# A hybrid gMLP and Mamba-2 trunk on one core: the head's sums move from GpSimd to VectorE and DMA, the decays' stores change queue, and the scans' chunk and the tail get another order

## The chip, the cores and the metric

One core of a Trainium2 chip runs the whole kernel. The metric is the device time of one execution, in microseconds (us). Five engines work beside each other, each through its own list of instructions in order: TensorE (PE, matmuls, with its weight loads shown as PEld), VectorE (DVE), ScalarE (ACT), GpSimd (POOL) and SyncE (SP, which only issues DMAs). ACT and POOL issue DMAs too. Semaphores tie the lists together.

## The reference

`x` is 1024 tokens by 1024 features in float32. Two layers add to it, and an RMSNorm ends the kernel.

```python
def spatial_gating_mixer(h, w_in, ln_w, ln_b, w_s, b_s, w_out):        # layer A
    z, u, v = jnp.split(h @ w_in, 3, axis=-1)                          # 1024 -> 3 x 2048
    v = layernorm(v, ln_w, ln_b)                                       # chunks of 128 tokens, 8 groups
    mixed = jnp.einsum('gts,bcsgd->bctgd', w_causal, v) + b_s...
    return (u * mixed * jax.nn.silu(z)) @ w_out

def ssd_mixer(h, ...):                                                 # layer B, Mamba-2
    z, xbc, dt_raw = ...split of h @ w_in                              # 2048, 4096, 32
    xbc = jax.nn.silu(causal_depthwise_conv(xbc, conv_w, conv_b))      # 4 taps
    x, Bm, Cm = ...xbc; dt = softplus(dt_raw + dt_bias)
    dA_cs = jnp.cumsum(dt * A, axis=2)                                 # in each chunk of 128
    w_ls = (Cm . Bm) * exp(cs_l - cs_s, causal) * dt
    y = w_ls @ x + (Cm @ prev state) * exp(dA_cs) + x * d_skip
    state = state * exp(dA_cs[-1]) + Bm^T (exp(dA_cs[-1] - dA_cs) * dt * x)
    gated = rmsnorm per group of 256 (y * silu(z))
    return gated @ w_out

h = x
h = h + spatial_gating_mixer(rmsnorm(h), ...)
h = h + ssd_mixer(rmsnorm(h), ...)
return rmsnorm(h)
```

## The kernel before

**Products.** Each float32 factor is split into a high half (a rounded copy, `hi`, on ACT) and a low half (the rest, `lo`, mostly on DVE), and each product is three matmuls: high by high, low by high, high by low (`mm3`, lines 134 to 136). On top of that every big product of a block is made with seven half-sized products in place of eight (Strassen's scheme in Winograd's form). So a `Block` has a left side `HS` of seven split matrices (A11, A12, A22 and the sums S1 to S4, `hh` and `hl` in the profile) and a right side of seven split weights (`wh`, `wl`), made of the raw quarters `b[kh, j]` (`wr`) and the sums t1, t2 (`t`).

**Stages.** `head()` (0 to about 92 us) loads x, normalizes it (`sq`, `rs_a`, `rs_b`, `norm`), transposes it (`tr`), forms the seven split matrices and runs the first block of v. The other v blocks run to about 220, the z and u blocks with the spatial mix to 525, the out-projection of layer A to 690, the step into layer B to 775. `blocks()` (to 1030) runs the z blocks and the xbc blocks of layer B, with the steps of `decays()` (softplus, cumulative sums, exp) and the convolution between their units. `scans()` (1033 to 1405) runs 8 groups of 8 chunks; between the chunks' small matmuls stand the projections of the groups still to come (`pj`, tile `ab`) and, in the last seven chunks, product 1 of the out-projection `bo`. `into_end()` runs the products 2, 7, 6, 4, 5, 3 of `bo` and the final norm.

**Order.** The kernel is written under a manual schedule: each engine executes in the order in which the code writes it. Semaphores only hold an instruction back. DMAs issued by SP and by ACT share eight semaphore lanes in turn, so such a DMA also waits for the one issued eight before it, whichever of the two queues issued that; POOL's DMAs have eight lanes of their own. An instruction that waits holds up all behind it on its engine.

**The head's sums.** `s1` to `s4` are the sums of the left side (F[t] holds the transposed rows t, in two halves), `again` rebuilds A12 from its halves, since F's half has been overwritten. t1, t2, the new b[1, 0] (B of product 4) and b[0, 1] (B of product 7) are four sums of weights. POOL does most of both kinds.

**The middle.** In `blocks()` a `unit` first takes one step of `decays()` (`next(small)`), then writes its matmuls. After the exponentials, eight stores write the cumulative sums and their exponentials to HBM (`cs_d`, `ecs_d`), from SP. `last` is a row of the tile that the `ecs_d` stores read.

**A chunk of the scans**, n of 64: `load` and `decay` (exp on ACT) and `tokens` (DVE) make the tiles of a chunk two ahead, `weights` (L1568, DVE) multiplies them one ahead, `pe_b` (L1577 and on, PE) uses them; `update` and `out` (DVE) take PE's result; `drain` runs steps of the convolution (L1282, DVE); `project` writes filler matmuls.

**The tail.** `sum_c`, `group_rstd` (`guess`, `tail`, `put`) and `rb` pass the last group's sums of squares through HBM: `ss_d`, `sv`, `rs_d`, `rb`. `hook_b(n, c)` writes these steps and the loads of the left side (`get`) between the units of `bo`'s products.

Of the kernel before, what the change touches and what calls it, by code (L numbers as in the profile page):

```python
# [29 lines left out]
def kernel(  # L30
# [149 lines left out]
    HS = new_H(("A11", "A12", "A22", "S1", "S2", "S3", "S4"))  # L180

    class Block:
# [104 lines left out]
        def post(self, n, i, parts=(0, 1)):  # L287
            a = self.acc[n][i]
            if n in (1, 6, 7) and 0 in parts:
                if i == 0:  # L290
                    self.u[n] = q4([P, 2, 512], "u")
                nc.scalar.copy(out=self.u[n][:, i], in_=a)  # L292
# [52 lines left out]
    def head():  # L345

        blk = v_block(0)
        V, S, G = nc.vector, nc.scalar, nc.gpsimd
        TTv, TTg = V.tensor_tensor, G.tensor_tensor
# [40 lines left out]
        def hi(name, t, src):  # L390
            S.copy(out=part(name, t)[0], in_=src)

        def lo(name, t, src):
            h_, l_ = part(name, t)
            TTv(out=l_, in0=src, in1=h_.bitcast(F32), op=ALU.subtract)  # L395

        def copy(t, kh):
            S.copy(out=F[t][:, kh], in_=TP[t][kh])
# [8 lines left out]
        def again(t):  # L407

            h_, l_ = part("A12", t)
            TTg(out=F[t][:, 1], in0=h_.bitcast(F32), in1=l_.bitcast(F32), op=ALU.add)  # L410

        def s3(t):
            TTg(out=F[t - 4][:, 0], in0=F[t - 4][:, 0], in1=F[t][:, 0], op=ALU.subtract)

        def s1(t, eng):
            eng(out=F[t][:, 0], in0=F[t][:, 0], in1=F[t][:, 1], op=ALU.add)

        def s2(t):
            TTv(out=F[t][:, 1], in0=F[t][:, 1], in1=F[t - 4][:, 0], op=ALU.subtract)

        def s4(t, eng=TTg):
            eng(out=F[t - 4][:, 1], in0=F[t - 4][:, 1], in1=F[t][:, 1], op=ALU.subtract)
# [3 lines left out]
        blk.t1, blk.t2 = t1, t2  # L426
        xp = [s8([P, 2, D], "xp") for _ in range(2)]
# [8 lines left out]
        for t in range(4, 8):  # L436
            load_x(t, q4([P, D], "xrow") if t < 7 else wr([P, D]))
# [14 lines left out]
        TTg(out=t1, in0=b[0, 1], in1=b[0, 0], op=ALU.subtract)
        TTg(out=t2, in0=b[1, 1], in1=t1, op=ALU.subtract)
# [3 lines left out]
        rs_a(4), rs_b(4), norm(4)  # L457
        hi("A11", 2, TP[2][0]), copy(2, 0), hi("A12", 2, TP[2][1])
        TTg(out=b[1, 0], in0=b[1, 0], in1=t2, op=ALU.subtract)
        TTg(out=b[0, 1], in0=b[1, 1], in1=b[0, 1], op=ALU.subtract)  # L460
        lo("A11", 2, TP[2][0]), lo("A12", 2, TP[2][1])
        hi("A11", 3, TP[3][0]), copy(3, 0), hi("A12", 3, TP[3][1])
        lo("A11", 3, TP[3][0]), lo("A12", 3, TP[3][1])
        norm(5)
        blk.mm(1, 1, False, (0,)), tr(4), blk.mm(1, 1, False, (1,))
        blk.mm(2, 1, False, (0,)), tr(5), blk.mm(2, 1, False, (1,))
        yhi(4, b[1, 0]), hi("A22", 4, TP[4][1]), copy(4, 1), sq(6), sq(7)
        ylo(4, b[1, 0]), lo("A22", 4, TP[4][1])
        copy(4, 0), rs_a(6), blk.post(2, 0), rs_b(6)
# [30 lines left out]
        ylo(5, t1, TTg)  # L500
        s4(4, TTv)
        for t in range(5, 8):
            s4(t)
# [704 lines left out]
    def decays():  # L1208
# [44 lines left out]
        last = dtw[:, 3, :]  # L1253
# [167 lines left out]
    def blocks():  # L1421
# [9 lines left out]
        small, turn, a21 = decays(), [0], rest_a21()  # L1431
# [7 lines left out]
        def unit(b, n, i):  # L1439
# [7 lines left out]
            elif next(small, 0) == 0 and todo and (turn[0] % 2 or len(todo) > 3):  # L1447
# [67 lines left out]
    class Scan:  # L1515
# [55 lines left out]
        def pe_b(self, c, ends=None):  # L1571
# [17 lines left out]
            if ends is not None:  # L1589
                ends.sum_b(sp[:, 256:512])  # L1590
# [68 lines left out]
        def sum_c(self, th):  # L1659
            (nc.sync if self.g < G - 1 else nc.scalar).dma_start(out=ss_d[self.g, th * 512:(th + 1) * 512].rearrange("(h t) -> h t", h=2),  # L1660
                              in_=self.sr[0:65:64])

    def group_rstd(g, t0, n):
# [4 lines left out]
        queue = nc.sync if g < G - 1 else nc.scalar  # L1668
        queue.dma_start(out=sv, in_=ss_d[g, t0:t0 + n].rearrange("(p c) -> p c", c=c))
# [11 lines left out]
        def put():  # L1681
            (nc.sync if g < G - 2 else nc.scalar).dma_start(out=rs_d[g, t0:t0 + n].rearrange("(p c) -> p c", c=c), in_=got[1])
# [287 lines left out]
```

## Time and profile before

| | |
|---|---|
| median of three runs | 1576.33 us (1572.9 to 1581.41) |
| the profiled execution | 1573.5 us, its span 1571.6 us |
| granted TensorE clock in it | 0.983 |
| PE busy | 1488.6 us (95%) |
| DVE, ACT, POOL busy | 1065.0, 782.2, 421.6 us |

How to read a row of the timeline: start, duration (us), engine (a q behind the name is the engine's own queue of DMA issues), line, operation, out <- in, and in brackets the idle time of the engine before it with what ended it. A row of a group gives the count, the busy time, and the mean of one in ns. A row of waits gives the sum, the count and the longest.

### The profile page before, as it was taken

The numbers are of one execution on the slowest core, as the hardware profiler recorded it, in microseconds if no ns is written. First come the engines' busy times: TensorE is split into PE (matmuls) and PEld (weight loads), VectorE is DVE, ScalarE is ACT, GpSimd is POOL, SyncE is SP. The second block draws the span as 40 slices with busy tenths as digits, with TensorE's granted clock in tenths as the row PEclk, the third lists the DMA queues.
The fourth block names the chain that finished last, engine by engine and source line by source line (L and its number), as shares of the span: only waits on it lengthen the run. The fifth ranks groups of instructions, "written<-read, shape, count | busy, mean of one in ns | idle before, by whom it ended". The sixth has DMA issues, their size and how long they took to land.

```text
span 1571.6 us, 21215 instructions
## 1 busy us (share of the span) xinstructions
PE 1488.6 (95%) x7830; PEld 1229.6 (78%) x7830; DVE 1065.0 (68%) x1701; ACT 782.2 (50%) x1251; POOL 421.6 (27%) x441
## 2 busy tenths in 40 slices
PE   5799999999999999999989999999999999987997
PEld 4799998888888888876768888777777776766876
DVE  7976566665666645778726477766776666776976
ACT  4523233322322445666546566656666756755463
POOL 3601110000000023211011313136776666532121
PEclk8999999999999999999999999999999999998999
DMA  5154333233322999947276988776566554678862
GB/s 176 42 185 137 108 99 112 99 107 104 108 92 87 356 243 240 242 126 160 94 166 147 184 176 164 174 230 196 139 169 182 161 158 132 209 261 175 232 129 107
DMA packets 174839, 251.82 MB, mean 160 GB/s; under 512 B 16288, under 2 KB 102928, under 8 KB 171536
## 3 DMA queue, kind: packets, MB, share of 16 engines
q1 hardware_dynamic: 124120, 168.39, 34.6%
q0 software_dynamic: 39520, 63.19, 20.7%
q10 hardware_dynamic: 11096, 18.90, 3.4%
q8 instruction: 62, 1.02, 0.3%
q14 instruction: 41, 0.34, 0.1%
HBM read 185.61 MB, written 51.18 MB: 151 GB/s over the span
## 4 chain that ended last, share of the span: by engine, by line
PE 63%; issue 15%; DVE 10%; ACT 6%; DMA 4%; POOL 1%; ACTq 0%; SPq 0%; POOLq 0%; DVEq 0%
PE acc L136 10%; PE acc L134 9%; PE acc L135 9%; PE ab L134 4%; PE ab L136 4%; PE ab L135 4%; PE ao L135 3%; PE ao L134 3%; PE ao L136 3%; PE yy L1577 2%; PE yy L1581 2%; DVE wl L112 2%; PE bo L135 2%; PE bo L134 2%; PE bo L136 2%
## 5 line engine op out<-in xcount | busy, mean ns | idle before, releaser
L134 PE MATMUL acc<-hh,wh 128*128 128x512 f32 x868 | 341.2, 393 | 7.7 <-ACT u L292 4.4
L136 PE MATMUL acc<-hh,wl 128*128 128x512 f32 x868 | 339.0, 391 | 1.4 <-DVE wl L112 1.4
L135 PE MATMUL acc<-hl,wh 128*128 128x512 f32 x868 | 338.4, 390 | 0.0
L112 DVE TENSOR_TENSOR wl<-wr,wh 128x1024 fp32r<-128x1024 f32 (+1 forms) x97 | 115.6, 1193 | 129.6 <-ACT wh L111 129.4
L134 PEld LDWEIGHTS acc<-hh,wh 128*128 128x128 f32 x868 | 163.5, 188 | 43.1 <-ACT u L292 6.0
L136 PEld LDWEIGHTS acc<-hh,wl 128*128 128x128 f32 x868 | 163.2, 188 | 37.6 <-DVE wl L112 3.7
L135 PEld LDWEIGHTS acc<-hl,wh 128*128 128x128 f32 x868 | 163.5, 188 | 33.1
L292 ACT COPY u<-acc 128x512 f32<-128x512 f32 x117 | 68.0, 583 | 207.1 <-PE acc L136 205.7
L111 ACT CAST wh<-wr 128x1024 fp32r<-128x1024 f32 (+1 forms) x113 | 116.4, 1030 | 98.4 <-PE acc L135 58.8
L136 PE MATMUL acc<-wh,hl 128*128 128x256 f32 x448 | 130.3, 291 | 12.2 <-DVE hl L395 12.1
L134 PE MATMUL ab<-hh,wh 128*128 128x512 f32 x288 | 129.1, 448 | 6.4 <-DVE x L1282 3.8
L134 PE MATMUL acc<-wh,hh 128*128 128x256 f32 x448 | 130.9, 292 | 3.9 <-DVE vt L331 2.5
L135 PE MATMUL acc<-wl,hh 128*128 128x256 f32 x448 | 129.6, 289 | 1.3 <-DVE wl L405 1.3
L136 PE MATMUL ab<-hh,wl 128*128 128x512 f32 x288 | 113.8, 395 | 0.0
L135 PE MATMUL ab<-hl,wh 128*128 128x512 f32 x288 | 112.9, 392 | 0.0
L136 PEld LDWEIGHTS acc<-wh,hl 128*128 128x128 f32 x448 | 88.7, 198 | 13.6 <-DVE hl L395 13.4
L134 PEld LDWEIGHTS acc<-wh,hh 128*128 128x128 f32 x448 | 88.7, 198 | 5.0 <-issue 2.9
L135 PEld LDWEIGHTS acc<-wl,hh 128*128 128x128 f32 x448 | 88.8, 198 | 1.7 <-DVE wl L405 1.5
L134 PE MATMUL bo<-wh,xh 128*128 128x512 f32 x192 | 77.7, 405 | 7.4 <-ACT wh L111 6.6
L112 DVE TENSOR_TENSOR xl<-ya,xh 128x1024 fp32r<-128x1024 f32 x40 | 49.8, 1246 | 51.2 <-ACT xh L111 51.2
L645 POOL DMA_DIRECT2D y_d<-y x8 | 4.4, 548 | 291.4 <-DVE y L642 291.4
L1550 ACT ACTIVATE wl<-wl,tk 128x128 f32<-128x128 f32 x256 | 81.5, 391 | 0.8 <-DMA wl<-cs_d 0.5
(320 smaller groups left out, 3284.3 us busy)
## 6 DMA issues: line engine op xcount, KB each, us to landing
wr<-in_a_w_in_dram SPq DMA_DIRECT2D x48, 512.0 KB, 3.6
wl<-cs_d SPq DMA_DIRECT2D x64, 256.0 KB, 3.5
wr<-in_b_w_in_dram SPq DMA_DIRECT2D x30, 512.0 KB, 7.3
wb<-in_a_w_out_dram SPq DMA_DIRECT2D x10, 1024.0 KB, 12.0
wb<-in_b_w_out_dram SPq DMA_DIRECT2D x10, 1024.0 KB, 7.7
wr<-in_b_w_in_dram SPq DMA_DIRECT2D x36, 256.0 KB, 7.2
v<-v_d SPq DMA_DIRECT2D x8, 1024.0 KB, 5.0
y_d<-y POOLq DMA_DIRECT2D x8, 1024.0 KB, 5.6
```

Of the source, the lines that this page charges most:

```text
L111: nc.scalar.copy(out=hi, in_=src)
L112: return (eng or nc.vector).tensor_tensor(out=lo, in0=src, in1=hi.bitcast(F32), op=ALU.subtract)
L134: nc.tensor.matmul(out=o, lhsT=l[0], rhs=r[0], start=start, stop=False, **kw)
L135: nc.tensor.matmul(out=o, lhsT=l[0], rhs=r[1], start=False, stop=False, **kw)
L136: nc.tensor.matmul(out=o, lhsT=l[1], rhs=r[0], start=False, stop=stop, **kw)
L292: nc.scalar.copy(out=self.u[n][:, i], in_=a)
L645: store = lambda: nc.gpsimd.dma_start(out=y_d[-1], in_=y)
L1550: nc.scalar.activation(wl[:, j, :], wl[:, j, :], AF.Relu, scale=-1.0, bias=tokc(2, c, self.g)[:, j:j + 1])
L1577: nc.tensor.matmul(out=yy[f * 64:(f + 1) * 64, pt * P:(pt + 1) * P], lhsT=w[:, j * 64:(j + 1) * 64], rhs=wl[:, j, :], start=True, stop=True)
L1581: nc.tensor.matmul(out=yy[:, 256 + pt * P:384 + pt * P], lhsT=self.state[c - 1][:, pt * P:(pt + 1) * P], rhs=self.x(3, c), start=True, sto ...
```

## The change

Four places of the code change, with the same products in the same order on PE.

*The head.* t1, t2, the new b[1, 0], s3, s1 and two low halves go to DVE. ACT copies A12's transposed rows into F as well, so that nothing rebuilds them. The rows 4 to 7 are copied with a minus sign, so that all sums are additions; S1 and S2 take the sign back in their halves. The new b[0, 1] is a scaling on ACT and an addition by DMA from HBM, and S4's sums are additions by DMA from SBUF, all in POOL's queue.

```diff
-            TTg(out=F[t][:, 1], in0=h_.bitcast(F32), in1=l_.bitcast(F32), op=ALU.add)
...
-            TTg(out=F[t - 4][:, 0], in0=F[t - 4][:, 0], in1=F[t][:, 0], op=ALU.subtract)
...
+        def sums(eng, *names):
+            for n, t in names:
+                a, c = {3: (F[t - 4][:, 0], F[t][:, 0]), 1: (F[t][:, 0], F[t][:, 1]),
+                        2: (F[t][:, 1], F[t - 4][:, 0]), 4: (F[t - 4][:, 1], F[t][:, 1])}[n]
+                if eng is None:
+                    nc.gpsimd.dma_start(out=a, in_=c, accum_op=ALU.add)
+                else:
+                    eng.tensor_tensor(out=a, in0=a, in1=c, op=ALU.add)
...
-        TTg(out=t1, in0=b[0, 1], in1=b[0, 0], op=ALU.subtract)
-        TTg(out=t2, in0=b[1, 1], in1=t1, op=ALU.subtract)
...
-        TTg(out=b[1, 0], in0=b[1, 0], in1=t2, op=ALU.subtract)
-        TTg(out=b[0, 1], in0=b[1, 1], in1=b[0, 1], op=ALU.subtract)
...
+        TTv(out=t1, in0=b[0, 1], in1=b[0, 0], op=ALU.subtract)
+        rs_b(4), norm(4)
...
+        norm(5), sq(6), sq(7), rs_a(6)
+        TTv(out=t2, in0=b[1, 1], in1=t1, op=ALU.subtract)
+        rs_b(6)
+        TTv(out=b[1, 0], in0=b[1, 0], in1=t2, op=ALU.subtract)
...
-        for t in (4, 5):
-            s3(t), s1(t, TTg)
-        yhi(6, t2)
+        sums(V, (3, 4), (3, 5), (1, 4), (1, 5))
+        S.mul(b[0, 1], b[0, 1], -1.0), blk.add(b[0, 1], 1, 1), yhi(6, t2)
...
-        s3(6), s1(6, TTg), s3(7)
+        sums(V, (2, 4), (2, 5), (3, 6), (1, 6))
...
+        sums(V, (3, 7), (1, 7), (2, 7), (2, 6)), sums(None, (4, 4), (4, 5))
...
+        sums(None, (4, 6), (4, 7))
```

*The middle.* The eight stores go to POOL's queue, `last` gets a tile of its own, and the step of `decays()` is taken behind the unit.

```diff
-            nc.sync.dma_start(out=cs_d[2 * q:2 * q + 2].rearrange("c h l -> h c l"),
+            nc.gpsimd.dma_start(out=cs_d[2 * q:2 * q + 2].rearrange("c h l -> h c l"),
...
-        last = dtw[:, 3, :]
+        last = k1([P, 256], "last")
...
-            elif next(small, 0) == 0 and todo and (turn[0] % 2 or len(todo) > 3):
+            elif done and todo and (turn[0] % 2 or len(todo) > 3):
...
             for f in off:
                 f()
+            if not done and next(small, 0) == 0:
+                done.append(True)
```

*The scans and the tail.* A chunk's steps are written in another order, and the last group's sum of squares is taken by two matmul steps more instead of a sum on POOL. The last group's small DMAs go from ACT's queue to SP's, and some hooks move.

```diff
-            if n >= N - 7:
-                k = n - N + 7
-                if k % 2:
-                    bo.prep(1, k // 2)
-                else:
-                    bo.ready(0, 0, k // 2)
             p = g if c >= 4 else g - 1
             at("pe_b", n, scan[p] if c % 4 == 3 and p >= 0 else None)
             project(want(n + .5))
             at("pe_a", n + 2)
-            at("update", n)
-            at("out", n)
             if n > 0:
                 at("weights", n + 1)
+            at("update", n)
+            at("out", n)
             at("decay", n + 2)
             at("carry", n + 1)
+            drain()
             at("tokens", n + 2)
             at("gate", n)
-            drain()
+            if n >= N - 7:
+                ...
...
-            (nc.sync if g < G - 2 else nc.scalar).dma_start(out=t[:, 0:n], in_=rs_d[g:g + n, th * 512:(th + 1) * 512].partition_broadcast(P))
+            nc.sync.dma_start(out=t[:, 0:n], in_=rs_d[g:g + n, th * 512:(th + 1) * 512].partition_broadcast(P))
...
         elif at == (1, 2):
-            for k in (0, 1):
-                get("a", 0, 1, k)
-            get("b", 1, 0, 0)
+            end["half"][0][0]()
         elif at == (1, 3):
-            end["half"] = [group_rstd(G - 1, 0, 512)]
             get("a", 0, 1, 2), get("b", 1, 0, 2)
+            end["half"][0][1](), end["half"][0][2]()
...
+        for k in (0, 1):
+            bo.get("a", 0, 1, k)
+        bo.get("b", 1, 0, 0)
         sc.sum_c(0), rs[G - 1][2]()
         sc.gate_half(1), sc.squares(1)
+        end["half"] = [group_rstd(G - 1, 0, 512)]
```

Three places show how the lists move. POOL in the head, before; `rr` is a step of the row norms, `xp`, `xrow` and `wr` the rows of x, `t_106` and `t_107` are t1 and t2:

```order
10 L141 TENSOR_TENSOR rr<-ss,mhalf 128x2 x2
11 L452 TENSOR_TENSOR t_106<-wr 128x1024
12 L453 TENSOR_TENSOR t_107<-wr,t_106 128x1024
13 L141 TENSOR_TENSOR rr<-ss,mhalf 128x2
14 L459 TENSOR_TENSOR wr<-wr,t_107 128x1024
15 L460 TENSOR_TENSOR wr<-wr 128x1024
16 L141 TENSOR_TENSOR rr<-ss,mhalf 128x2
17 L413 TENSOR_TENSOR xp<-xp,xrow 128x512
18 L416 TENSOR_TENSOR xrow<-xrow 128x512
```

and after:

```order
8 masks.py:199 AFFINE_SELECT ident<-ident 128x128
9 L167 AFFINE_SELECT mask<-ones 128x128
10 L141 TENSOR_TENSOR rr<-ss,mhalf 128x2 x4
11 L202 DMA wr<-in_a_w_in_dram 128x4x256
12 L423 DMA xp<-xrow 128x512 x4
13 L335 DMA v_d_93<-vt 128x512 x2
```

Of POOL's sums in the head nothing is left but the four small `rr`; the additions by DMA stand behind them. On DVE, t1 and t2 now stand between the steps of the row norms (`ru`, `rs`, `ss`) and the splits (`hl`):

```order
28 L401 TENSOR_TENSOR hl<-tp,hh 128x4x128 x4
29 L375 SCALAR_TENSOR_TENSOR xrow<-xrow,rs,nwb 128x512 x2
30 L364 TENSOR_SCALAR ss<-ss 128x2
31 L467 TENSOR_TENSOR t_105<-wr,t_104 128x1024
32 L150 TENSOR_TENSOR ru<-rr 128x2
33 L599 TENSOR_SCALAR hv<-hv 128x1
34 L151 TENSOR_TENSOR ru<-ru,ss 128x2
35 L152 TENSOR_SCALAR ru<-ru 128x2
36 L153 TENSOR_TENSOR rs<-rr,ru 128x2
37 L469 TENSOR_TENSOR wr<-wr,t_105 128x1024
38 L415 TENSOR_TENSOR wl<-wr,wh 128x1024
```

Row 31 is t2, row 37 the weights of product 4, row 38 their low half. The second place is ACT's list in the middle, with what each instruction waits for (`DMAHW` is a lane of SP's and ACT's DMAs); before:

```order
402 L977 ACTIVATE zt<-zt 128x512 [waits DMAHW4_49,DVE_49]
403 L978 DMA z_d_5289<-zt 128x512 [waits DMAHW7_49,Activation_49]
404 L111 CAST wh<-wr 128x1024 [waits PE_49]
405 L977 ACTIVATE zt<-acc 128x512 [waits DMAHW6_49,PE_49]
406 L978 DMA z_d_5288<-zt 128x512 [waits DMAHW4_49,Activation_49]
407 L1255 COPY dtw<-dtw 128x128 x2
408 L977 ACTIVATE zt<-acc 128x512 [waits DMAHW5_49,PE_49]
409 L978 DMA z_d_5288<-zt 128x512 [waits DMAHW6_49,Activation_49]
410 L111 CAST wh<-wr 128x1024 [waits DMAHW0_49]
411 L1263 COPY tk<-tp 128x256 [waits PE_49]
```

and after:

```order
410 L976 ACTIVATE zt<-zt 128x512 [waits DMAHW4_49,DVE_49]
411 L977 DMA z_d_5290<-zt 128x512 [waits Activation_49]
412 L111 CAST wh<-wr 128x1024 [waits PE_49]
413 L976 ACTIVATE zt<-acc 128x512 [waits DMAHW6_49,PE_49]
414 L977 DMA z_d_5289<-zt 128x512 [waits Activation_49]
415 L976 ACTIVATE zt<-acc 128x512 [waits DMAHW2_49,PE_49]
416 L977 DMA z_d_5289<-zt 128x512 [waits Activation_49]
417 L1254 COPY last<-dtw 128x128 x2
418 L111 CAST wh<-wr 128x1024 [waits DMAHW0_49]
```

The z_d stores no longer wait for a lane. The third place is DVE's list in the scans, one chunk and a little more (L1558 and L1560 are `tokens`, L1568 `weights`, L1607 `update`, L1619 and L1622 `out`, L1282 a tap of the convolution); before:

```order
923 L1568 TENSOR_TENSOR wl<-wl,cw 128x512
924 L1558 TENSOR_TENSOR cw<-tp,tk 128x256
925 L1560 TENSOR_TENSOR cw<-tp,mask 128x128
926 L1282 SCALAR_TENSOR_TENSOR bc<-ab,par,bc 128x1023
927 L1607 TENSOR_TENSOR state<-sp,state 128x256
928 L1619 TENSOR_TENSOR t_9421<-yy,ze 128x256
929 L1622 SCALAR_TENSOR_TENSOR cw<-x,dsk,yy 128x128 x2
930 L1568 TENSOR_TENSOR wl<-wl,cw 128x512
```

and after, where each of these lines is one higher but the tap's, which is one lower:

```order
924 L1569 TENSOR_TENSOR wl<-wl,cw 128x512
925 L1608 TENSOR_TENSOR state<-sp,state 128x256
926 L1620 TENSOR_TENSOR t_9371<-yy,ze 128x256
927 L1623 SCALAR_TENSOR_TENSOR cw<-x,dsk,yy 128x128 x2
928 L1281 SCALAR_TENSOR_TENSOR bc<-ab,par,bc 128x1023
929 L1559 TENSOR_TENSOR cw<-tp,tk 128x256
930 L1561 TENSOR_TENSOR cw<-tp,mask 128x128
931 L1569 TENSOR_TENSOR wl<-wl,cw 128x512
```

The weights now stand ahead of the state and the output, and the tap ahead of the tokens.

More of the change, by code (lines that the diff above doesn't have):

```diff
@@ L179 @@
     xr = x.rearrange("(c p) d -> c p d", p=P)
-    HS = new_H(("A11", "A12", "A22", "S1", "S2", "S3", "S4"))
+    HS = new_H(("A11", "A12", "A22", "S1", "S2", "S3"))
     class Block:
@@ L289, in post @@
             if n in (1, 6, 7) and 0 in parts:
-                if i == 0:
+                if i == 0 and n not in self.u:
                     self.u[n] = q4([P, 2, 512], "u")
@@ L390, in hi @@
         def hi(name, t, src):
-            S.copy(out=part(name, t)[0], in_=src)
+            h_ = part(name, t)[0]
+            if name in MINUS:
+                S.mul(h_, src, -1.0)
+            else:
+                S.copy(out=h_, in_=src)
         def lo(name, t, src):
             h_, l_ = part(name, t)
-            TTv(out=l_, in0=src, in1=h_.bitcast(F32), op=ALU.subtract)
+            if name in MINUS:
+                V.scalar_tensor_tensor(l_, src, -1.0, h_.bitcast(F32), ALU.mult, ALU.subtract)
+            else:
+                TTv(out=l_, in0=src, in1=h_.bitcast(F32), op=ALU.subtract)
         def copy(t, kh):
-            S.copy(out=F[t][:, kh], in_=TP[t][kh])
+            if t < 4:
+                S.copy(out=F[t][:, kh], in_=TP[t][kh])
+            else:
+                S.mul(F[t][:, kh], TP[t][kh], -1.0)
         def yhi(n, src, eng=S.copy):
@@ L405, in ylo @@
             eng(out=blk.Y[n][1], in0=src, in1=blk.Y[n][0].bitcast(F32), op=ALU.subtract)
-        def again(t):
-            h_, l_ = part("A12", t)
-            TTg(out=F[t][:, 1], in0=h_.bitcast(F32), in1=l_.bitcast(F32), op=ALU.add)
-        def s3(t):
-            TTg(out=F[t - 4][:, 0], in0=F[t - 4][:, 0], in1=F[t][:, 0], op=ALU.subtract)
[L415 to L422, printed above, removed]
+        def sums(eng, *names):
[4 more added lines that the diff above has]
+                    nc.gpsimd.dma_start(out=a, in_=c, accum_op=ALU.add)
+                else:
+                    eng.tensor_tensor(out=a, in0=a, in1=c, op=ALU.add)
         b = blk.b
@@ L499, in head @@
             lo("S3", t, F[t - 4][:, 0])
[L500 to L503, printed above, removed]
+        ylo(5, t1)
         for i in range(2):
@@ L516, in head @@
             nxt.load(kh, j)
+        HS.update(new_H(("S4",)))
         for t in range(4, 8):
@@ L1430, in blocks @@
         seq = [(k, n) for k in range(len(bs)) for n in (ORDER if k < len(bs) - 1 else LAST)]
-        small, turn, a21 = decays(), [0], rest_a21()
+        small, turn, a21, done = decays(), [0], rest_a21(), []
         def ahead(at):
@@ L1659, in sum_c @@
         def sum_c(self, th):
[L1660 removed]
+            nc.sync.dma_start(out=ss_d[self.g, th * 512:(th + 1) * 512].rearrange("(h t) -> h t", h=2),
                               in_=self.sr[0:65:64])
@@ L1667, in group_rstd @@
         sv = tiny([P, 8], "sv")[:, 0:c]
-        queue = nc.sync if g < G - 1 else nc.scalar
-        queue.dma_start(out=sv, in_=ss_d[g, t0:t0 + n].rearrange("(p c) -> p c", c=c))
+        nc.sync.dma_start(out=sv, in_=ss_d[g, t0:t0 + n].rearrange("(p c) -> p c", c=c))
         got = []
@@ L1681, in put @@
         def put():
-            (nc.sync if g < G - 2 else nc.scalar).dma_start(out=rs_d[g, t0:t0 + n].rearrange("(p c) -> p c", c=c), in_=got[1])
+            nc.sync.dma_start(out=rs_d[g, t0:t0 + n].rearrange("(p c) -> p c", c=c), in_=got[1])
         return guess, tail, put
@@ L1739, in hook_b @@
             get("b", 0, 1, 0)
-            end["half"][0][0]()
             last.sum_b(n=2)
@@ L1863, in scans @@
                 bo.get("b", 0, 0, 0)
+            p = g if c >= 4 else g - 1
+            at("pe_b", n, scan[p] if c % 4 == 3 and p >= 0 else None)
+            project(want(n + .5))
+            at("pe_a", n + 2)
+            if n > 0:
+                at("weights", n + 1)
+            at("update", n)
+            at("out", n)
+            at("decay", n + 2)
+            at("carry", n + 1)
+            drain()
+            at("tokens", n + 2)
+            at("gate", n)
             if n >= N - 7:
@@ L1869, in scans @@
                     bo.ready(0, 0, k // 2)
-            p = g if c >= 4 else g - 1
-            at("pe_b", n, scan[p] if c % 4 == 3 and p >= 0 else None)
-            project(want(n + .5))
-            at("pe_a", n + 2)
-            at("update", n)
-            at("out", n)
-            if n > 0:
-                at("weights", n + 1)
-            at("decay", n + 2)
-            at("carry", n + 1)
-            at("tokens", n + 2)
-            at("gate", n)
-            drain()
             at("load", n + 3)
```

59 lines of the change are left out of this document (24 added, 35 removed).

## The prediction

> **What bounds the kernel now.** I read the page's shares first, then the chain, then TensorE's waits stretch by stretch, and last the rows around each wait.
>
> ```profile
> span 1571.6 us, 21215 instructions
> PE 1488.6 (95%) x7830; PEld 1229.6 (78%) x7830; DVE 1065.0 (68%) x1701; ACT 782.2 (50%) x1251; POOL 421.6 (27%) x441
> PE 63%; issue 15%; DVE 10%; ACT 6%; DMA 4%; POOL 1%; ACTq 0%; SPq 0%; POOLq 0%; DVEq 0%
> ```
>
> TensorE (PE) is busy 1488.6 of 1571.6 us. The change takes no product away, so it can only win from the other 83 us, and from matmuls that run slowly because the clock has been taken down after a wait. Four stretches hold most of both: the head, the middle, the scans and the tail.
>
> ```profile
> 9.60:83.30 73.70, 53.42 (x354) 50.69 (x354) 67.42 (x79) 39.01 (x69) 37.79 (x23) 0.86 0.30 95
> 1229.00:1234.00 5.00, 5.00 (x23) 4.12 (x24) 1.87 (x5) 4.97 (x8) 2.25 (x2) 0.68 1.00 250
> 1399.00:1405.00 6.00, 5.71 (x27) 3.90 (x28) 5.87 (x12) 0.72 (x2) 4.63 (x4) 0.72 0.99 351
> ```
>
> The columns after the window are its length, the busy time of PE, its weight loads, DVE (VectorE), ACT (ScalarE) and POOL (GpSimd), then PE's granted clock. In the head PE idles 73.7 - 53.4 = 20.3 us and runs at 0.86, so some 53.4 x 0.14 = 7.5 us more are slow clock; DVE, busy 67.42 of 73.70, is the engine that is full. The other two windows follow PE waits of 1.90 and 2.62 us (rows in C): 0.68 over 5 us and 0.72 over 6 us mean about 1.6 us lost again after each such wait.
>
> The Trainium skill, page "TensorE: Matmul & The Clock Gate", Part 1, puts the step down to half clock behind an idle window of about 3.4 us. The two rows show it behind shorter waits; by the page's rule only the waits over 3.4 us would give clock back, and the whole gain would be some 5 us smaller than the sum below. The sum goes by the rows.
>
> **A, the head.** The change takes 20 tensor operations off POOL: 12 go to DVE, four become copies on ACT, four become additions by DMA.
>
> ```profile
> 16.07 2.38 POOL L452 TENSOR_TENSOR t<-wr 128x1024 f32<-128x1024 f32 x1 [1.39 <-DMA wr<-in_a_w_in_dram]
> 16.37 2.09 DVE L150 TENSOR_TENSOR ru<-rr 128x2 f32<-128x2 f32 x1
> 18.50 0.16 DVE L151 TENSOR_TENSOR ru<-ru,ss 128x2 f32<-128x2 f32 x1
> L395 DVE TENSOR_TENSOR hl<-xrow,hh 128x512 fp32r<-128x512 f32 x6 | 10.0, 1711 | 0.9 <-ACT hh L391 0.9
> L395 DVE TENSOR_TENSOR hl<-tp,hh 128x512 fp32r<-128x512 f32 x12 | 7.9, 684 | 0.4 <-ACT xrow L398 0.3
> L419 DVE TENSOR_TENSOR xrow<-xrow,xp 128x512 f32<-128x512 f32 x3 | 5.7, 1939 | 0.0
> L150 DVE TENSOR_TENSOR ru<-rr 128x2 f32<-128x2 f32 x4 | 5.3, 1337 | 1.6 <-POOL rr L141 1.6
> L152 DVE TENSOR_SCALAR ru<-ru 128x2 f32<-128x2 f32 x4 | 3.7, 928 | 0.1
> L151 DVE TENSOR_TENSOR ru<-ru,ss 128x2 f32<-128x2 f32 x4 | 2.8, 692 | 0.1
> L405 DVE TENSOR_TENSOR wl<-wr,wh 128x1024 fp32r<-128x1024 f32 x4 | 4.9, 1218 | 0.0
> ```
>
> A DVE operation on 128x2 takes 0.16 us (18.50), but 2.09 us when it starts inside POOL's 2.38 us sum (16.37): the two engines exclude each other. The groups give the price: six low halves of S1/S2/S4 at 1711 ns against 684 for the same shape from PSUM, 6.2 us; three sums at 1939 against about 690, 3.7 us; the twelve tiny ones 11.8 us against 1.9, 9.9 us; single rows of the same kind, not shown, another 4.8 us. About 24.6 us of DVE's 67.4 is such waiting, and goes with POOL's sums. Added to DVE: five 128x1024 operations (t1, t2, B10's sum, two low halves) at 1.22 and seven 128x512 at 0.69, less one S4 sum of 0.69: 10.2 us. So DVE has 67.4 - 24.6 + 10.2 = 53 us of work, PE 46 at full clock, in a stretch that is now 73.7 long.
>
> It doesn't shrink to 53, since operations wait for each other. Walking the new order row by row with these durations, the low halves of A11/A12 of rows 2 and 3 are done 7 us earlier, but the weights of product 4, behind t2, B10's sum, copy and split (now all on DVE and ACT), only 1.2 us; product 6 starts 10 us earlier, and product 3, from which PE now runs without a wait, 13 us earlier.
>
> ```profile
> PE acc L136 <- DVE hl L395: 12.1, 4, 3.6
> wb<-wb POOLq DMA_DIRECT2D x12, 512.0 KB, 15.0
> f<-f POOLq DMA_DIRECT2D x2, 512.0 KB, 5.3
> ```
>
> 12.1 us of the idle time are the low halves (hl) alone, so most of 13 is there to be taken. ACT gets four copies of 128x512 and a scaling of 128x1024, some 3.5 us at the 1.04 us that it takes for 128x1024 (807.63 below) and a little over half of that for the smaller, beside 39.0 of 73.7 busy: nothing on the path while DVE is the fuller. The additions by DMA in POOL's queue are B01's (from HBM) and four for S4 (SBUF to SBUF; one of these sums was DVE's). Neither kind stands in the head now; the nearest are SBUF additions of 512 KB, 5.3 and 15.0 us from issue to landing. S4's four, of 256 KB each, go out at 50 to 57 and are wanted at about 66, so 5.3 costs nothing and 15.0 from the last costs about 6 us. I take -10: the walk's 13 less half of that. Bounds +1 (only product 4's 1.2 us is won, and additions of 15.0 us hold products 7 and 3 up by two) and -14.
>
> **B, the middle.** The stores of the decays leave SP's queue for POOL's.
>
> ```profile
> 779.87 0.68 DVE L972 TENSOR_TENSOR zt<-acc,u 128x512 f32<-128x512 f32 x1
> 783.20 0.50 PE L134 MATMUL acc<-hh,wh 128*128 128x512 f32 x1 [3.12 <-ACT u L292]
> 802.23 0.49 ACT L1255 COPY dtw<-dtw 128x128 f32<-128x128 f32 x2 [4.57 <-DMA ecs_d<-dtw]
> 807.26 0.33 ACTq L978 DMA_DIRECT2D z_d<-zt  x1
> 807.63 1.04 ACT L111 CAST wh<-wr 128x1024 fp32r<-128x1024 f32 x1 [4.40 <-DMA cs_d<-cs]
> 809.00 0.69 PE L1260 MATMUL tp<-ident,cs 128*128 128x128 f32 x2 [5.95 <-ACT tk L1263]
> 818.53 1.26 POOL L202 DMA_DIRECT2D wr<-in_b_w_in_dram  x1 [22.62 <-ACT tk L1265]
> ```
>
> ACT stands still for 4.57 and 4.40 us at a DMA that it issues itself (a z_d store): in the order with its semaphores, each such store waits on a lane that SP's cs_d and ecs_d stores hold, since the DMAs of SP and ACT share eight lanes in turn. PE waits 5.95 us for it, and I count 1.4 us of slow clock behind that, a little under the windows above. With the stores in POOL's queue, which has lanes of its own, the same z_d rows wait for ACT alone. The other wait, 3.12 us at 783.20, is a z block's DVE operation (779.87) behind the decays' chain on DVE; the chain's steps now come behind a unit's matmuls and its z operation. The walk gives 5.95 + 1.4 + 3.1 = 10.5. Against it: eight issues of 1.26 us on POOL, 10 us in all, beside an idle stretch of 22.62, but now ahead of weight loads in the same queue. I take -9, bounds 0 and -10.5.
>
> **C, the scans.** Each of 64 chunks gets a new order on DVE: weights first, and product 1's splits last.
>
> ```profile
> PE yy L1577 <- issue: 8.4, 6, 3.3
> PE ab L134 <- DVE x L1282: 3.8, 2, 1.9
> PE yy L1577 <- DVE wl L1568: 2.6, 1, 2.6
> PE ab L134 <- DVE bc L1282: 1.9, 1, 1.9
> 1396.04 1.22 DVE L112 TENSOR_TENSOR wl<-wb,wh 128x1024 fp32r<-128x1024 f32 x1
> 1399.29 1.04 PE L1577 MATMUL yy<-wl,cw 128*64 128x128 f32 x8 [2.62 <-DVE wl L1568]
> 1225.94 1.27 DVE L1282 SCALAR_TENSOR_TENSOR x<-ab,par,x 128x1021 f32<-128x1021 f32 x1
> 1227.26 0.50 PE L134 MATMUL ab<-hh,wh 128*128 128x512 f32 x1 [1.90 <-DVE x L1282]
> ```
>
> 16.7 us of waits. Those for a convolution tap (L1282, 5.7 us) come from a tap that runs after decay and mask of the chunk; drain now precedes tokens, so the tap moves up by 0.9 us or more: 4.4, and two slow clocks, 3.2. Of yy's 11 us, the last group's 6 (3.29 at 1387, 2.62 at 1399) are weights behind a split of product 1; the split now stands behind the chunk: 5, with 1.7 of clock. Elsewhere 4 of the rest. Sum 18. But a wait of DVE for exp in front of the weights now holds update and out too, and the split at a chunk's end can delay the next chunk's weights by its 1.22 us. So I take -11, bounds +4 and -20.
>
> **D, the tail.** The last group's tiny DMAs go from ACT's queue to SP's, and sooner.
>
> ```profile
> 1435.61 0.33 ACTq L1694 DMA_DIRECT2D rb<-rs_d  x1
> 1435.99 1.92 ACT L711 ACTIVATE wb<-wb 128x2048 f32<-128x2048 f32 x1 [4.98 <-DMA sv<-ss_d]
> 1442.53 0.79 PE L134 MATMUL bo<-wh,xh 128*128 128x512 f32 x1 [5.46 <-ACT wh L111]
> rb<-rs_d SPq DMA_DIRECT2D x6, 512.0 KB, 5.9
> ```
>
> ACT's queue waits 4.98 us for sv, then issues rb; PE waits 5.46 for the split that follows. With rb in SP's queue, by the walk some 15 us sooner, the wait goes, and a slow clock of 1.6 us behind it: 7. Given back: SP now holds half 0's rs_d, which waits for DVE at about 1415, ahead of the next rb and ya loads; those took 1401 to issue before and would now go at 1416, landing 5.9 us later (the SP row) at 1422 to 1424, when DVE wants them at 1422. Walk 6; I take -4, bounds +4 and -9. The small waits elsewhere stay, and so does the end.
>
> **Sum.** -10 - 9 - 11 - 4 = -34 on the profiled 1573.5 (span 1571.6 and 1.9 around it): 1539.5. The median of the runs is 2.8 above the profiled one, so I put the number at 1541, 2.2% faster.
>
> **Rivals.** *Weights first makes DVE wait (slower).* DVE works in order; if exp is late by w in each chunk, all behind it shifts and PE ends up waiting 64 x w. This row shows such a wait, just behind one of ACT's table loads:
>
> ```profile
> 1116.36 0.71 DVE L1568 TENSOR_TENSOR wl<-wl,cw 128x512 f32<-128x512 f32 x1 [0.65 <-ACT wl L1552]
> ```
>
> At 0.65 in every chunk, 41.6 us replace the 11: 1541 + 11 + 42 = 1594, slower. A, B and D win 23, so it makes the kernel slower from 23 / 64 = 0.36 us in every chunk on. Against it: ACT is 50% busy, and only the chunks behind a table load have such a wait now.
>
> *The gain is given back in part.* The head stays on the chain of product 4 (-4), the splits at a chunk's end eat half of the scans' part (-5), SP's waits in the tail all of its 4: with the middle's 9 that is -18, 1557.
>
> *The walk holds everywhere:* -13 - 10.5 - 18 - 6 = -47.5, 1528.
>
> *DMAs from POOL starve.* If the landing of S4's additions or the decays' stores is held off by DVE, as POOL's sums hold off DVE now, A and B win nothing: -15, 1560. The Trainium skill, page "SBUF — State Buffer", section "Who interferes with whom", lets a DVE operation in a two-port mode keep GpSimd from writing descriptors; no row of before shows a DMA held so.
>
> **How the numbers follow.** The sum as taken (1530 to 1551): 0.52. The walk in full (1523 to 1530): 0.12. Given back (1551 to 1563): 0.15; starved: 0.08. Weights-first waits: 0.07. The rest, gains and losses near zero: 0.06. 1523 to 1563 holds the first three and most of the fourth, 0.84, and leaves out the last two. About 0.5% (8 us) is what can be told from no change, so faster, below 1568, is 0.87; same 0.06; slower 0.07.
>
> **What would show it.** Right: no DVE operation of 128x2 over 0.2 us in the head, PE's run without waits begins near 70; no ACT gap of 4 us before a z_d store; PE waits before the scans' weights products (yy) under 6 us in total; no 5 us wait near 1440. Wrong: weights that wait for exp in most chunks; S4's high half waiting for a DMA; POOL's weight loads landing after their cast; a PE wait behind rb or ya at product 7.

## The result, and the profile after

The changed kernel takes 1533.75 us in the median (1531.71 to 1535.45), the kernel before 1574.62 in the same comparison: a ratio of 0.9734, 95% interval 0.9699 to 0.977, so 2.7% faster. The forecast was 1541, with a range of 1523 to 1563. The page after the change, the span, the shares, and the granted clock in 40 slices:

```profile
span 1530.0 us, 21278 instructions
PE 1478.6 (97%) x7834; PEld 1218.4 (80%) x7834; DVE 1054.6 (69%) x1712; ACT 784.1 (51%) x1256; POOL 392.2 (26%) x433
PEclk9999999999999999999999999999999999999999
```

The span fell by 41.6 us. PE's idle time fell from 83 to 51.4 us and its busy time by 10, though it does the same products: fewer matmuls run at a low clock (the mean granted clock rose from 0.983 to 0.998). Since PE's order is the same in both kernels, the start of the same matmul can be compared. The views of four tiles (ao: layer A's out-projection; ab: the scans' projections; yy: the chunks; bo with yh: the last product) have the first and the last start after the three durations; before, then after:

```profile
L134 PE MATMUL ao<-wh,xh x192: 389/389/476, 546.2 to 677.9; 128*128 128x512 f32 x192
L134 PE MATMUL ab<-hh,wh x288: 387/397/931, 1024.5 to 1372.1; 128*128 128x512 f32 x144
L1577 PE MATMUL yy<-wl,cw x512: 272/273/476, 1047.6 to 1399.9; 128*64 128x128 f32 x171
L134 PE MATMUL bo<-yh,wh x32: 389/389/468, 1541.2 to 1562.4; 128*128 128x512 f32 x32
```

```profile
L134 PE MATMUL ao<-wh,xh x192: 389/389/476, 532.8 to 664.5; 128*128 128x512 f32 x192
L134 PE MATMUL ab<-hh,wh x288: 387/397/586, 1004.2 to 1339.9; 128*128 128x512 f32 x144
L1578 PE MATMUL yy<-wl,cw x512: 272/273/324, 1027.3 to 1361.2; 128*64 128x128 f32 x171
L134 PE MATMUL bo<-yh,wh x32: 387/389/468, 1499.6 to 1520.8; 128*128 128x512 f32 x32
```

From the start to the first ao (the head lies in it) 13.4 us are won, by the first ab (the middle) 20.3, by the last yy (the scans) 38.7, by the last product (the tail) 41.6. So the four parts brought 13.4, 6.9, 18.4 and 2.9. In the table below the middle is counted from the last matmul of ao in line 134 (706.3 before, 692.9 after, of a row that is not shown) to the first ab, the scans from the first to the last yy, the tail from there to the start of the last product; us, from the profile of each kernel in the experiments:

| kernel | median | head, to first ao | middle | scans | tail |
|---|---|---|---|---|---|
| before | 1574.62 | 546.2 | 318.2 | 352.3 | 141.3 |
| after | 1533.75 | 532.8 | 311.3 | 333.9 | 138.4 |
| undo_head | 1545.45 | 547.2 | 309.9 | 334.2 | 138.7 |
| undo_middle | 1542.31 | 532.4 | 319.8 | 334.3 | 139.4 |
| undo_chunk | 1547.86 | 532.9 | 314.0 | 352.3 | 134.6 |
| undo_tail | 1538.11 | 533.1 | 312.8 | 333.9 | 142.4 |
| pool_reads | 1545.19 | 544.5 | 311.6 | 334.5 | 138.5 |
| pool_writes | 1533.52 | 533.1 | 314.7 | 333.9 | 139.2 |
| stores_sp | 1539.90 | 531.8 | 317.1 | 334.2 | 138.7 |
| three_stores | 1533.68 | 532.1 | 313.9 | 333.9 | 138.7 |
| splits_first | 1537.50 | 533.4 | 315.2 | 338.2 | 136.9 |
| weights_late | 1539.43 | 531.7 | 312.4 | 342.1 | 136.2 |
| drain_last | 1541.78 | 532.6 | 311.7 | 338.8 | 139.4 |
| splits_mid | 1531.61 | 532.1 | 312.8 | 332.9 | 138.5 |

Where nothing was touched, head, scans and tail repeat within 1.7, 0.6 and 1.0 us; the middle spreads from 309.9 to 315.2 (mean 312.6) in the ten kernels with the same middle, so a difference of 5 us there is not read from one profile. The stretches are those of one execution of each kernel. That execution is 2.0 us below its kernel's median in the changed kernel, 4.0 below in drain_last and 2.7 above in undo_chunk. The changed kernel was not run again beside the experiments, and the kernel before took 1574.62 to 1578.37 us in the medians of the comparisons; a difference of medians of 2 us therefore says little.

### The profile page after: what moved, and what is told of

Same layout as the page of the kernel before. It is cut to its first block, busy times and chain, and to the rows that moved or that the text cites. A ratio compares the mean times of both kernels' runs of the same rounds, so it can differ in the third digit from the quotient of the medians.

```text
span 1530.0 us, 21278 instructions
## 1 busy us (share of the span) xinstructions
PE 1478.6 (97%) x7834; PEld 1218.4 (80%) x7834; DVE 1054.6 (69%) x1712; ACT 784.1 (51%) x1256; POOL 392.2 (26%) x433
## 5 line engine op out<-in xcount | busy, mean ns | idle before, releaser
L135 PE MATMUL bo<-wl,xh 128*128 128x512 f32 x192 | 76.1, 396 | 7.3 <-DVE wl L112 7.2
```

The costliest lines, as they stand in the source:

```text
L135: nc.tensor.matmul(out=o, lhsT=l[0], rhs=r[1], start=False, stop=False, **kw)
```

## The experiments

**Each part undone alone.** Four kernels, each the changed one with one part as before. Their edits are the lines of the change, taken back: the head's functions; the stores' queue, `last` and the place of the step; the order of a chunk; the queues and hooks of the last group. The last group's sum by matmul in place of GpSimd's is taken back in none of them.

> The changed kernel with the head as before (sums on GpSimd), all else changed. Theory (DVE was held up by GpSimd's sums in the head, and each part's gain stays in its own stage): 13.4 us come back, so about 1547 us against 1533.8, all before the first out-projection matmul (533 to 546). Rival (the four stages gain together, through buffers and lanes that the head hands on): the time differs by under 8 or over 18 us, or stages behind the head move by over 2 us.

Measured 1545.45, +11.7 in the medians, and 14.4 in the head's stretch alone, with nothing behind it later by more. The theory holds: the gain stays in its stage.

> The changed kernel with the decays' eight stores in SP's queue again and the step ahead of each unit. Theory (ACT's z_d stores wait on the stores' lanes): ACT's two waits of over 4 us and PE's 5.9 us wait come back, 6.9 us, so about 1541. Rival (the wait hangs on the head's timing and was not B's to win): under 3 us, 1537 or less.

Measured 1542.31, +8.6; the middle takes 319.8 us. PE's two waits are back, the second with 3.7 us in place of 5.95, in the view of PE's waits. ACT's two are back in its timeline, and its rows name the stores again:

```profile
PE acc L134 <- ACT u L292: 4.2, 3, 3.1
PE tp L1259 <- ACT tk L1262: 3.7, 1, 3.7
```

```profile
788.86 0.50 ACT L1254 COPY dtw<-dtw 128x128 f32<-128x128 f32 x2 [3.65 <-DMA ecs_d<-dtw]
794.57 1.04 ACT L111 CAST wh<-wr 128x1024 fp32r<-128x1024 f32 x1 [4.71 <-DMA cs_d<-cs]
```

> The changed kernel with the chunk's old order in the scans (splits of product 1 first, weights behind state and output, drain last). Theory (PE's waits before the weights products and the taps come from this order): 16 us of PE waits and 1.6 us of slow clock behind each of the longer ones come back, 18 us, so about 1552. Rival (the waits went because the last group's sum left GpSimd and the DMAs moved): under 8 us, 1542 or less.

Measured 1547.86, +14.1. The scans take 352.3 us, as before to a tenth, 18.4 more; but the tail takes 3.8 less: PE's waits in it, nearly all for splits, are 6.1 us against 9.8. So in sum the new chunk is worth 14, not 18: part of what it wins it gives back in the tail. That the splits of product 1 come sooner is only part of the reason, since with that move alone undone the tail is 1.5 us shorter, and with the weights' move alone 2.2 (splits_first and weights_late, below).

> The changed kernel with the last group's small DMAs in ACT's queue and the hooks where they were. Theory: the 5 us wait of PE near 1442 comes back and the five new waits of 0.5 to 1 us at product 2 go, net 3 us, so about 1537. Rival (the new small waits are worth as much as the wait that went): within 1 us of 1534.

Measured 1538.11, +4.4, and 4.0 in the tail: a little above the theory's 3. The small waits did not go: ahead of the large one PE still waits five times for a split, 0.85 to 1.15 us each. PE's large wait is back:

```profile
1406.95 0.80 PE L134 MATMUL bo<-wh,xh 128*128 128x512 f32 x1 [5.45 <-ACT wh L111]
```

The head's 14.4, the middle's 8.5, the scans' 18.4 less 3.8 and the tail's 4.0 add up to 41.5, beside the 41.6 of the spans. That they fit so well is luck: by stage the undone parts give 14.4, 8.5, 18.4 and 0.2, where 13.4, 6.9, 18.4 and 2.9 were won. In the tail the parts depend on each other: its change is worth 6.7 us with the chunk's old order (141.3 to 134.6) and 4.0 with the new one (142.4 to 138.4). By the medians the four parts are 11.7, 8.6, 14.1 and 4.4, in sum 38.7 of 40.9.

**What slowed the head: GpSimd's reads.** Two kernels put idle work on GpSimd into the changed head, on a tile that nobody reads any more:

```diff
         norm(5), sq(6), sq(7), rs_a(6)
+        for _ in range(3):
+            nc.gpsimd.tensor_tensor(out=side[:, 0], in0=side[:, 0], in1=side[:, 0], op=ALU.add)   # pool_reads
+        for _ in range(8):
+            nc.gpsimd.memset(side[:, 0], 0.0)                                                     # pool_writes
```

and the same behind B01's addition.

> The changed kernel with six sums of 128x1024 on GpSimd that nothing needs, over a tile in SBUF that is free by then, three behind the row norms and three behind B01's addition: some 14 us of GpSimd time where it is idle. Theory (DVE cannot run while GpSimd reads SBUF): DVE's small operations and sums beside them are stretched by up to 2.4 us each, DVE's list gets 8 to 13 us later, and product 3 starts 5 to 11 us later: 1539 to 1545. Rival (the head was slow because products waited for GpSimd's results, not because of sharing): within 2 us of 1534.

> The changed kernel with sixteen memsets of the same 128x1024 tile on GpSimd at the same two places: GpSimd is busy and writes SBUF, but reads nothing. Theory (only GpSimd's reads exclude a DVE operation with two inputs): DVE's operations keep their lengths, and the time stays within 2 us of 1534 unless the memsets take so long that B01's addition or S4's go out late. Rival (any GpSimd work beside it slows DVE): stretched rows as with the sums, 1539 or more.

pool_reads took 1545.19, +11.4; pool_writes 1533.52, no difference. Timeline of pool_reads, GpSimd, DVE and PE, then of pool_writes, GpSimd and DVE:

```profile
33.17 5.84 POOL L468 TENSOR_TENSOR side<-side 128x1024 f32<-128x1024 f32 x3
33.23 1.85 DVE L150 TENSOR_TENSOR ru<-rr 128x2 f32<-128x2 f32 x1 [0.59 <-POOL rr L141]
35.31 1.75 DVE L152 TENSOR_SCALAR ru<-ru 128x2 f32<-128x2 f32 x1
37.17 2.92 DVE L471 TENSOR_TENSOR wr<-wr,t 128x1024 f32<-128x1024 f32 x1
42.70 0.58 PE L134 MATMUL acc<-wh,hh 128*128 128x256 f32 x1 [7.45 <-ACT xrow L408]
44.93 7.19 DVE L375 SCALAR_TENSOR_TENSOR xrow<-xrow,rs,nwb 128x512 f32<-128x512 f32 x4
```

```profile
32.27 8.01 POOL L468 MEMSET side<- 128x1024 f32 x8
32.74 0.50 DVE L152 TENSOR_SCALAR ru<-ru 128x2 f32<-128x2 f32 x1
33.35 1.22 DVE L471 TENSOR_TENSOR wr<-wr,t 128x1024 f32<-128x1024 f32 x1
39.41 2.73 DVE L375 SCALAR_TENSOR_TENSOR xrow<-xrow,rs,nwb 128x512 f32<-128x512 f32 x4
```

Six useless sums stretch the four norm operations from 2.73 to 7.19 us and product 4's weights from 1.22 to 2.92. With `ru` (1.85 and 1.75 us, against 0.16 and 0.17 in the changed kernel) and a pair of sums (2.98 against 1.28, not shown), DVE's rows are 11.1 us longer, and the head's stretch is 11.7 us longer. B01's addition goes out 5.5 us later too, since it waits for ACT and ACT for DVE. Sixteen memsets, 16.6 us of GpSimd, leave the same two rows as they are. So GpSimd's being busy does not slow the head, and GpSimd reading SBUF beside DVE does, without anything waiting for its results. How much of the 13.4 us won in the head is this, and how much is products that had waited for GpSimd's results, the two runs don't separate. The stretched operations with two inputs in SBUF agree with the Trainium skill, page "SBUF — State Buffer", section "Who interferes with whom": a DVE instruction with two SBUF inputs contends with a GpSimd instruction that reads SBUF, not with one that only writes it. The one row that the memsets did stretch, 0.50 us against 0.17, is a tensor_scalar with one input, which the sums stretched as well (1.75); its two-port mode the same section names.

**The middle, the queue apart from the step.** The stores go back to SP, the step stays behind the unit (`nc.gpsimd.dma_start` to `nc.sync.dma_start` for cs_d and ecs_d):

> The changed kernel, but the decays' eight stores are in SP's queue again; the step stays behind the unit. Theory (of the middle's two waits the one of 3.1 us is the step's and the one of 5.9 us the queue's): the middle takes 316 to 317 us against 311.3, ACT waits for cs_d and ecs_d again, PE's wait of 3.1 us for a z operation stays away; 1539 in all. Rival (the queue does it all, the step nothing): the middle takes 319 or more.

Measured 1539.90; the middle takes 317.1. The wait at a z operation stays away, the other is back, in the timelines of PE and ACT:

```profile
794.58 0.69 PE L1259 MATMUL tp<-ident,cs 128*128 128x128 f32 x2 [4.48 <-ACT tk L1262]
791.78 0.50 ACT L1254 COPY last<-dtw 128x128 f32<-128x128 f32 x2 [4.79 <-DMA wr<-in_b_w_in_dram]
```

ACT again stands still at a z_d store, but its row names a weight load of SP's queue, not cs_d or ecs_d as expected: the lane was held by another DMA of SP's queue. So the queue is worth 5.8 us against the profile after, or 4.5 against the mean of the ten kernels that share the new middle (312.6), and 6.2 in the medians. The step is worth 1.1 to 2.7 us, which is less than one profile can tell here; but its wait stays away while the other is back, so one wait belongs to each.

**What is left of the middle.** The eight stores are written as three larger ones in GpSimd's queue:

```diff
-        for q in range(4):
-            ...two stores, of cs and of ecs, for 32 rows
+        for c in range(2):
+            nc.gpsimd.dma_start(out=cs_d.rearrange("(q c) h l -> c q h l", c=2)[c], in_=cs[:, c * P:(c + 1) * P])
+        yield
+        nc.gpsimd.dma_start(out=ecs_d.rearrange("h (q t) -> q h t", q=4), in_=ecs)
```

> The changed kernel with the decays' eight stores in GpSimd's queue written as three larger ones with the same contents. Theory (what is left of the middle's loss, some 2.5 us of small PE waits and ACT's wait of 6.5 us for a weight load, is the eight stores in front of weight loads and on lanes of the same queue): the middle takes 309 us against 311.3, 1531 to 1532 in all. Rival (the weight loads are late by themselves): 311 to 312, no change.

Measured 1533.68, the middle 313.9: no gain. ACT's wait for a weight load is 6.8 us, against 6.5 in the changed kernel, and the three stores land as late (17.8 and 18.0 us) as the eight (below). That alone leaves open whether the stores delay the load. The kernel above with no store in GpSimd's queue, stores_sp, settles it: the load that ACT waits for lands there 17.4 us after its issue, against 18.3 in the changed kernel. So all but 0.9 us of it the load is late by itself. Its issue in stores_sp, then in the changed kernel, from the lists of DMA issues around it:

```profile
t<-in_b_w_in_dram POOLq DMA_DIRECT2D x1, 512.0 KB, 17.4
```

```profile
t<-in_b_w_in_dram POOLq DMA_DIRECT2D x1, 512.0 KB, 18.3
```

**The chunk's three moves, one undone each.** Against the changed kernel's order (weights, update, out, decay, carry, drain, tokens, gate, splits): splits_first puts the block `if n >= N - 7` back ahead of `pe_b`, and the two others move one step each.

```diff
-            if n > 0:
-                at("weights", n + 1)
             at("update", n)
             at("out", n)
+            if n > 0:
+                at("weights", n + 1)     # weights_late
...
-            drain()
             at("tokens", n + 2)
             at("gate", n)
+            drain()                      # drain_last
```

> The changed kernel, but in the last seven chunks of the scans the splits of product 1 stand first in the chunk again. Theory (each of the three moves in the chunk pays for its own waits): the last group's weights wait behind the splits again, two waits of 2.6 and 3.3 us and slow clock behind them, so the scans' stretch is 340 us against 333.9, and the tail 135 against 138.4, since the splits come sooner; 1537 in all. Rival (one move, the weights ahead of the output, does nearly all): the scans stay within 2 us of 333.9.

> The changed kernel, but the scans' weights stand behind state and output again. Theory (each move pays its own): PE waits before a chunk's weights product about where it did, 4 to 6 us in all, so the scans take 339 us; 1539 in all. Rival (one move does nearly all): 345 us or more, 1546 in all. Other rival (the weights ahead of the output make DVE wait for exp, 12 waits and 15.7 us now, so the old place is better): under 333.

> The changed kernel, but the convolution's steps stand at the chunk's end again. Theory (each move pays its own): the three waits of 1.9 us for a tap come back with slow clock behind two of them, so the scans take 342 us; 1542 in all. Rival (the weights move does nearly all): within 2 us of 333.9.

Measured: 1537.50, scans 338.2, tail 136.9; 1539.43, scans 342.1, tail 136.2; 1541.78, scans 338.8, tail 139.4. In the scans they lose 4.3, 8.2 and 4.9 us, 17.4 together, of the 18.4 that undoing all three loses. Each move pays for its own waits, and none does it all. The weights' own part, 8.2, lies between the theory's 5 and the rival's 11. The tap's is below the theory's 8 in the profile, but the profiled execution of drain_last, 1537.79 us at a clock of 0.996, is the fastest of four; the others took 1541.06 to 1544.02 at 0.991 to 0.993, and in the medians the move costs 8.0. The tail gets 1.5 and 2.2 us shorter with the first two undone and 1.0 longer with the third. PE's waits in the last seven chunks (splits_first), and in the scans (weights_late, drain_last, two rows):

```profile
1356.76 1.12 PE L1578 MATMUL yy<-wl,cw 128*64 128x128 f32 x8 [2.24 <-ACT wl L1551]
1369.66 0.66 PE L1578 MATMUL yy<-wl,cw 128*64 128x128 f32 x8 [1.84 <-DVE wl L1569]
```

```profile
PE yy L1578 <- issue: 6.6, 6, 1.7
```

```profile
PE ab L134 <- DVE x L1281: 3.8, 2, 1.9
PE ab L134 <- DVE bc L1281: 1.9, 1, 1.9
```

**A place between.** Since the splits first shorten the tail and lengthen the scans, the last run puts them behind `out` and ahead of `decay`:

```diff
             at("out", n)
+            if n >= N - 7:
+                ...bo.prep or bo.ready, as before
             at("decay", n + 2)
```

> The changed kernel, but in the last seven chunks the splits of product 1 stand between the output and the decay, so that ScalarE casts them ahead of the exponentials of the chunk two ahead. Theory (with the splits first the tail was 1.5 us shorter than with them last, and the scans 4.3 us longer only because the weights stood behind them; between the two places the tail keeps its part and the weights theirs): scans 333 to 334, tail 137, 1531 to 1533 in all. Rival (exponentials and tokens that come 2 us later make PE wait for the weights two chunks on): scans 335 or more, no gain.

Measured 1531.61 (ratio 0.9718, interval 0.9698 to 0.9738), scans 332.9, tail 138.5. The wait of 0.75 us in the scans for a split's low half is gone, so the scans win 1.0 us; the tail doesn't get its part. The intervals of this kernel and of the changed one overlap, so that it is faster isn't shown.

## Why the prediction was right, step by step

*The bound.* Right: all the gain is PE's idle time and slow clock. The four stretches were the right ones: 41.6 us in them, and none elsewhere (between these two kernels the stretches between them and the end differ by less than 0.1 us).

*A, the head.* -10 taken, -13.4 measured; the walk's 13 was right and the discount wrong. The window to 70 us after the change, some DVE rows, product 3's first matmul, and the landing of S4's additions:

```profile
9.60:70.00 60.40, 49.37 (x351) 46.86 (x352) 53.21 (x92) 40.71 (x73) 9.22 (x8) 0.97 0.53 146
16.54 0.15 DVE L150 TENSOR_TENSOR ru<-rr 128x2 f32<-128x2 f32 x1
35.73 1.23 DVE L415 TENSOR_TENSOR wl<-wr,wh 128x1024 fp32r<-128x1024 f32 x1 [1.11 <-ACT wh L412]
70.47 0.28 PE L134 MATMUL acc<-wh,hh 128*128 128x256 f32 x1
xp<-xrow POOLq DMA_DIRECT2D x4, 256.0 KB, 5.5
```

DVE's work is 53.2 us, as worked out; `ru` takes 0.15 us in place of 2.09; product 4's weights are ready 1.4 us earlier (forecast 1.2), product 3 starts at 70.47 instead of 83.34 (forecast 13 earlier). The term that was mis-sized is the additions by DMA: 5.5 us from issue to landing, the lower of the two rows that bounded them, not half way to 15.0; PE does not wait for them. The rival of starving DMAs needs a DVE that holds them off; here nothing of the kind shows.

*B, the middle.* -9 taken, -6.9 measured (by undoing it 8.5, or 7.2 against the mean of the ten). The lane mechanism is shown: with the stores in SP's queue ACT's waits come back, and in undo_middle they name the stores. The term that was too small is what is left, though one profile tells it only within the spread of the middle: new small PE waits, 2.4 us in sum, and ACT's stall at a weight load of GpSimd's queue, which the prediction named as a sign of being wrong; PE shows 0.78 us of it. They stand in the timelines of ACT, PE and POOL and the list of DMA issues:

```profile
799.44 1.04 ACT L111 CAST wh<-t 128x1024 fp32r<-128x1024 f32 x1 [6.47 <-DMA t<-in_b_w_in_dram]
800.53 0.50 PE L134 MATMUL acc<-hh,wh 128*128 128x512 f32 x1 [0.78 <-ACT wh L111]
794.45 0.53 POOL L1245 DMA_DIRECT2D cs_d<-cs  x1 [5.18 <-DMA t<-in_b_w_in_dram]
cs_d<-cs POOLq DMA_DIRECT2D x4, 32.0 KB, 16.5
```

GpSimd's queue waits on lanes of its own now (794.45), and a store of 32 KB lands after 16.5 us; but only GpSimd's own queue waited for it (4.71 us). Larger and fewer stores changed neither (three_stores). Whether the weight load itself can come sooner was not tried and stays open.

*C, the scans.* -11 taken, -18.4 measured; the walk's 18 was right. The discount, DVE standing at exp in front of the weights, is real but harmless, as the views of DVE's waits (first row) and of PE's show:

```profile
DVE wl L1569 <- ACT wl L1553: 15.7, 12, 3.1
PE ab L134 <- DVE x L1281: 1.1, 2, 0.7
PE yy L1578 <- issue: 0.4, 1, 0.4
```

DVE waits 15.7 us in twelve chunks, against 0.7 in one before, while PE's waits in the scans, these two rows, one of 0.7 for a split and one of 0.5, are 2.7 us in all, against 17.7 before. So 15.0 of the 18.4 us are waits and 3.4 clock, where the walk has 13.4 and 4.9. Undone one by one, drain, splits and weights lose 4.9, 4.3 and 8.2 in the profiles, where the walk has 7.6, 6.7 and 4: the causes were right, but that the sum met is in part luck. The rival that this makes the kernel slower priced each wait of DVE as one of PE; between the weights and PE's use of them there is slack. What the prediction did not foresee is the 3.8 us that the new chunk costs the tail.

*D, the tail.* -4 taken, -2.9 measured; 4.0 by undoing it, the rest being what the chunk's order gives back here. The cause of the 5.46 us wait was right. The give-back named was wrong: no PE wait follows from rs_d in SP's queue. In its place stand waits of the splits, since ACT casts two tiles and DVE makes two low halves one after the other for each unit, PE after the change:

```profile
1372.61 0.49 PE L134 MATMUL bo<-wh,xh 128*128 128x512 f32 x1 [0.85 <-ACT wh L111]
1374.06 0.50 PE L135 MATMUL bo<-wl,xh 128*128 128x512 f32 x1 [0.96 <-DVE wl L112]
1386.33 0.50 PE L135 MATMUL bo<-wl,xh 128*128 128x512 f32 x1 [0.95 <-DVE wl L112]
```

With the long wait gone, the splits of a unit are what PE waits for at product 2. The chunk's new order has its part in them: with the tail as before they stand too (undo_tail), and with the chunk as before four are left, of 0.49 to 0.96 us (undo_chunk).

*The sum.* 34 forecast, 41.6 in the profile: A and C won 3.4 and 7.4 us more than was taken, B and D 2.1 and 1.1 less. The walk in full, 47.5, was 5.9 off on the other side.

## What to carry to other kernels

Before giving GpSimd work because it idles, look at what DVE does in that stretch: a sum on GpSimd that reads SBUF held up DVE's operations with two inputs there for as long as it ran (`ru` took 1.85 us beside three sums of 5.84 us), while memsets cost the head nothing. An ACT or SP instruction that waits at its own DMA may be waiting on a lane held by the other queue's DMA: the row names the DMA, the order with its semaphores the lane. And a walk through the new order with durations from the rows was within 10% in the two largest stages, in the scans with terms that were off both ways; taking it down for DMAs or waits whose slack was not counted made the forecast worse there.

## What the runs showed of the hardware that was not expected

The same PE wait is followed by a slow clock in one run and not in another. A wait of 1.90 us for a tap, in the kernel before, in drain_last, and in undo_chunk, which has the chunk's order of before, with matmuls that follow:

```profile
1269.63 0.74 PE L134 MATMUL ab<-hh,wh 128*128 128x512 f32 x1 [1.90 <-DVE bc L1282]
1270.17 0.63 PE L135 MATMUL ab<-hl,wh 128*128 128x512 f32 x1
```

```profile
1244.68 0.50 PE L134 MATMUL ab<-hh,wh 128*128 128x512 f32 x1 [1.90 <-DVE bc L1281]
1245.01 0.39 PE L135 MATMUL ab<-hl,wh 128*128 128x512 f32 x1
```

```profile
1253.92 0.40 PE L135 MATMUL ab<-hl,wh 128*128 128x512 f32 x1
1294.81 0.63 PE L135 MATMUL ab<-hl,wh 128*128 128x512 f32 x1
```

0.63 us for the next matmul in the first, 0.39 in the second. Of the three waits of 1.90 us, the first two are followed by slow matmuls in the kernel before, none in drain_last, and in undo_chunk the first and the third: its second (1253.92) is not, its third (1294.81) is from the fourth matmul on. So the profiled execution of drain_last lost 4.9 us in the scans where the waits alone are 4.6, and the 3.2 us of clock that the prediction counted with them is no fixed price. The Trainium skill, page "TensorE: Matmul & The Clock Gate", Part 1, has a free-running window of activity of about 3.4 us; a window that runs free would explain why the same wait is punished at one time and not at another, though no run here shows where the window stood, and the 1.90 us show that a wait shorter than the window can be punished.
